# The low half of each weight tile by a negated copy and an accumulating DMA, in a one-core decoder layer

## The chip, the core and the metric

One core of one Trainium2 chip runs the program. The metric is the device time of one execution in microseconds (us). Before the change three runs took 771.84, 771.36 and 771.56 us; the median is 771.56 us.

## What is computed

One layer of a decoder, 512 tokens wide 1024, all in float32:

```
u = rms_norm(h, norm_mix_pre);  proj = u @ w_in          # 1024 -> 10*256 + 4*1024
y_a, y_b, y_c, y_d = four token mixers on slices of proj # 512 x 256 each
merged = sum_k sigmoid(gate_k) * (y_k @ w_branch[k])      # 512 x 1024
h = h + rms_norm(merged @ w_out, norm_mix_post)
u = rms_norm(h, norm_mlp_pre)
hid = square(relu(u @ w_up))                              # 512 x 4096
h = h + rms_norm(hid @ w_down, norm_mlp_post)
```

## The kernel before, in words

**Products in three parts.** Each float32 operand is split into a high half, rounded to the type that TensorE reads (float32r), and a low half, the rest. `mm3` (lines 180 to 183) makes a product of two operands from three matmuls: high by high (L181), then the two mixed ones (L182, L183). So every weight tile is needed twice, as `whi` and as `wlo`, each [128, 1024].

**Units.** The weights lie in DRAM as 132 units of [128, 1024] (512 KB) in the order of use. A unit goes through three steps. `load` (L129) sends its DMA from SyncE's queue into one of 3 `raw` buffers. `prep` (L143) takes one of 6 `whi` and one of 6 `wlo` buffers and calls `split` (L139): ScalarE copies `raw` to `whi` (L140), then VectorE writes `wlo = raw - whi` (L141). Then TensorE uses the pair, 24 matmuls of 512 columns for a unit. `unit()` (L172) prepares 4 units ahead of the one that it hands out. Units 66 and 67 go to a spare pair of buffers of another pool.

**Stages.** Ten slots of the input projection (20 units), then four gates (40 units, 8 of them of `w_branch`), with the mixers' own steps written between them; then `w_out` (8 units); then the MLP in 8 groups of 512 hidden columns. A group is `up_group`, which uses four units one after the other, and `down_group` of the group before, which holds four units together: each of its 8 output pieces takes 3 matmuls from each of the four (12 matmuls), and VectorE adds the piece to `macc` (L918). In `up_out` ScalarE applies relu (L850), VectorE squares (L851), and `split` makes the halves of `hid`.

**The end.** The last `down_group` also forms row sums (ScalarE L738, VectorE L749), the norm, the gain (GpSimd L926) and the residual, and sends the output.

**Order.** A scheduler orders each engine's instructions when the program is built, and each engine runs its own queue in order. So ScalarE's copy for a unit stands at a fixed place among its other work, and what stands behind it waits with it. GpSimd has little to do before the last group: memsets, and one cast (L250).

Of the kernel before, what the change touches and what calls it, by code (L numbers as in the profile page):

```python
# [12 lines left out]
AF = mybir.ActivationFunctionType  # L13
ALU = mybir.AluOpType
# [35 lines left out]
def tile_hybrid_trunk(ctx: ExitStack, tc: tile.TileContext, xT, xn, wts, par, bd, cst, msk, gains, out):  # L50
    nc = tc.nc
    act, dve, pool, pe = nc.scalar, nc.vector, nc.gpsimd, nc.tensor
# [15 lines left out]
    def nm(s):  # L68
        cnt[0] += 1
        return f"{s}_{cnt[0]}"  # L70
# [19 lines left out]
    def y_pair():  # L90
        r = []
        for s in ("hi", "lo"):
            r.append(yp.tile([P, 2 * T], F32R, tag="y", name=nm("y" + s)))
        return r
# [23 lines left out]

    NU = wts.shape[0]
    SPARE = (66, 67)  # L120
    spare = []
    LOADCUT = {0: ((0, 256), (256, 512), (512, D))}
    xfirst = [0, 1, 2]

    def xload(k):
        nc.sync.dma_start(xt[k // 2][:, k % 2], xT[k])

    def load(n):
        while Wt.n_load < min(n, NU):  # L129
            i = Wt.n_load  # L130
            r = rp.tile([P, D], F32, tag="raw", name=nm("raw"))
            for o, e in LOADCUT.get(i, ((0, D),)):
                if i == 0 and xfirst:
                    xload(xfirst.pop(0))
                nc.sync.dma_start(r[:, o:e], wts[i, :, o:e])
            Wt.raw[i] = r
            Wt.n_load += 1

    def split(hi, lo, src):  # L139
        act.activation(hi, src, AF.Copy)  # L140
        dve.tensor_tensor(lo, src, hi.bitcast(F32), ALU.subtract)  # L141

    def prep(n):  # L143
        while Wt.n_prep < min(n, NU):
            i = Wt.n_prep
            load(i + 1)
            r = Wt.raw.pop(i)
            if i in SPARE:
                if not spare:
                    spare.extend(up.tile([P, 2, D], F32R, tag="u", name=nm("sp")) for _ in range(2))  # L150
                hi, lo = (x_[:, i - SPARE[0]] for x_ in spare)
            else:
                hi = wp.tile([P, D], F32R, tag="whi", name=nm("whi"))
                lo = wp.tile([P, D], F32R, tag="wlo", name=nm("wlo"))
            for o, e in LOADCUT.get(i, ((0, D),)):
                if i == 0 and xorder[0] == 0:
                    xorder.pop(0)
                    xsplit(0, lambda: split(hi[:, o:e], lo[:, o:e], r[:, o:e]))
                    continue
                split(hi[:, o:e], lo[:, o:e], r[:, o:e])  # L160
                if i == 0:
                    xsplit(xorder.pop(0))
            Wt.hl[i] = (hi, lo)
            Wt.n_prep += 1
            load(i + 3)
# [6 lines left out]
    def unit():  # L172
        i = use[0]
        use[0] += 1
        prep(i + ahead[0])
        if extra:
            extra.pop(0)()
        return Wt.hl.pop(i)
# [27 lines left out]
    def xsplit(k, between=None):  # L206
        src = xt[k // 2][:, k % 2]
        g = prm("gmix", k)
        if k == 0:
            dve.tensor_scalar(U(uh, k), src, g, None, ALU.mult)  # L210
        else:
            act.activation(U(uh, k), src, AF.Copy, scale=g)  # L212
        if between:
            between()
        dve.scalar_tensor_tensor(U(ul, k), src, g, U(uh, k).bitcast(F32), ALU.mult, ALU.subtract)  # L215
# [11 lines left out]
    for k in range(4, NK):  # L227
        xload(k)
    load(3)
    prep(1)  # L230
    xsplit(3)
    prep(2)
    for k in range(4, NK):
        xsplit(k)
# [135 lines left out]
    hi, lo = y_pair()  # L370
# [688 lines left out]
```

## Time and profile before

| | |
|---|---|
| three runs, us | 771.84, 771.36, 771.56 |
| span of the profiled execution, us | 769.9 |
| TensorE (PE) busy | 756.5 us, 98% |
| VectorE (DVE) busy | 450.2 us, 58% |
| ScalarE (ACT) busy | 264.5 us, 34% |
| GpSimd (POOL) busy | 18.8 us, 2% |
| mean granted TensorE clock | 0.996 |
| DMA | 80.40 MB, mean 104 GB/s |

The profile gives the profiled execution as its span, from the first to the last instruction; the page lists no other time for it. The chain that ended last consists of PE for 95% of the span. A busy PE is one with a matmul in flight, since matmuls overlap.

### The profile page before, as it was taken

What the parts mean: (1) busy time and instruction counts of PE and PEld (TensorE: products, weight loads), DVE (VectorE), ACT (ScalarE), POOL (GpSimd) and SP (SyncE); (2) the same over time, 40 slices, a digit from 0 to 9 for tenths busy, and PEclk for the clock granted to TensorE, in tenths of its full rate; (3) what the DMA queues carried; (4) which work ended last, traced back from release to release, by engine and by line L of the source; (5) the groups of instructions that cost most, each with busy time, mean ns of one, the idle gap of its engine ahead of it and who ended that gap; (6) DMA issues with size and microseconds to landing.
All of it is one profiled execution on the core that took longest, in us unless ns stands there. A gap on an engine that the chain in (4) does not pass through costs nothing.

```text
span 769.9 us, 9006 instructions
## 1 busy us (share of the span) xinstructions
PE 756.5 (98%) x3592; PEld 636.0 (83%) x3592; DVE 450.2 (58%) x699; ACT 264.5 (34%) x375; POOL 18.8 (2%) x21
## 2 busy tenths in 40 slices
PE   8999999999999999999999999999999999999994
PEld 7888988888888888888889988888888888888883
DVE  5798246559988476465476742435354453435357
ACT  6524122337223223234242743413142231414123
POOL 1100000000000000000000000000000000000014
PEclk9999999999999999999999999999999999999998
DMA  8732223132222263233321331405142331405002
GB/s 338 247 116 98 98 94 110 56 109 83 83 82 68 97 219 110 82 102 118 109 82 56 117 104 53 139 28 163 55 140 79 109 111 34 157 28 163 28 1 109
DMA packets 23945, 80.40 MB, mean 104 GB/s; under 512 B 2784, under 2 KB 3552, under 8 KB 23904
## 3 DMA queue, kind: packets, MB, share of 16 engines
q1 hardware_dynamic: 23616, 79.67, 30.9%
q8 instruction: 28, 0.46, 0.3%
q10 hardware_dynamic: 288, 0.17, 0.1%
q14 instruction: 13, 0.11, 0.0%
HBM read 77.73 MB, written 2.10 MB: 104 GB/s over the span
## 4 chain that ended last, share of the span: by engine, by line
PE 95%; DVE 3%; DMA 1%; ACT 0%; issue 0%; DVEq 0%; ACTq 0%
PE mm L182 22%; PE mm L183 22%; PE mm L181 22%; PE sm L181 9%; PE sm L183 8%; PE sm L182 8%; PE sm L512 2%; DMA raw<-in_wts_dram 1%; DVE stat L749 1%; DVE macc L918 0%; DVE t L896 0%; PE sm L621 0%; DMA par_s<-in_par_dram 0%; PE sm L807 0%; DVE nt L762 0%
## 5 line engine op out<-in xcount | busy, mean ns | idle before, releaser
L140 ACT ACTIVATE whi<-raw 128x1024 fp32r<-128x1024 f32 (+1 forms) x132 | 136.8, 1046 | 334.0 <-PE mm L182 138.6
L141 DVE TENSOR_TENSOR wlo<-raw,whi 128x1024 fp32r<-128x1024 f32 (+1 forms) x132 | 158.7, 1207 | 135.2 <-ACT whi L140 134.8
L182 PE MATMUL mm<-ul,whi 128*128 128x512 f32 x384 | 149.3, 390 | 0.6 <-DVE ul L215 0.6
L181 PE MATMUL mm<-uh,whi 128*128 128x512 f32 x384 | 148.7, 392 | 0.9 <-ACT uh L212 0.9
L183 PE MATMUL mm<-uh,wlo 128*128 128x512 f32 x384 | 149.1, 390 | 0.0
L182 PE MATMUL mm<-u2l,whi 128*128 128x512 f32 (+1 forms) x288 | 105.2, 366 | 0.0
L183 PE MATMUL mm<-u2h,wlo 128*128 128x512 f32 (+1 forms) x288 | 105.0, 365 | 0.0
L181 PE MATMUL mm<-u2h,whi 128*128 128x512 f32 (+1 forms) x288 | 104.4, 365 | 0.0
L182 PE MATMUL sm<-wlo,hid 128*128 128x512 f32 (+1 forms) x260 | 100.3, 386 | 0.0
L183 PE MATMUL sm<-whi,hid 128*128 128x512 f32 (+1 forms) x260 | 100.3, 386 | 0.0
L181 PE MATMUL sm<-whi,hid 128*128 128x512 f32 (+1 forms) x260 | 100.0, 386 | 0.0
L182 PEld LDWEIGHTS mm<-ul,whi 128*128 128x128 f32 x384 | 72.3, 188 | 16.0 <-DVE ul L215 1.2
L181 PEld LDWEIGHTS mm<-uh,whi 128*128 128x128 f32 x384 | 72.2, 188 | 16.0 <-ACT uh L212 1.3
L183 PEld LDWEIGHTS mm<-uh,wlo 128*128 128x128 f32 x384 | 72.1, 188 | 15.0
L918 DVE TENSOR_TENSOR macc<-macc,sm 128x512 f32<-128x512 f32 (+1 forms) x57 | 38.3, 676 | 71.3 <-PE sm L183 71.3
L183 PEld LDWEIGHTS mm<-u2h,wlo 128*128 128x128 f32 x288 | 54.3, 189 | 8.8
L182 PEld LDWEIGHTS mm<-u2l,whi 128*128 128x128 f32 x288 | 54.3, 189 | 8.7
L181 PEld LDWEIGHTS mm<-u2h,whi 128*128 128x128 f32 x288 | 54.0, 189 | 8.8
L183 PEld LDWEIGHTS sm<-whi,hid 128*128 128x128 f32 x260 | 48.8, 188 | 9.9
L181 PEld LDWEIGHTS sm<-whi,hid 128*128 128x128 f32 x260 | 48.8, 188 | 9.8
L182 PEld LDWEIGHTS sm<-wlo,hid 128*128 128x128 f32 x260 | 48.8, 188 | 9.8
L851 DVE TENSOR_TENSOR s<-s 128x512 f32<-128x512 f32 x32 | 22.0, 688 | 37.8 <-ACT s L850 37.8
(242 smaller groups left out, 788.1 us busy)
## 6 DMA issues: line engine op xcount, KB each, us to landing
raw<-in_wts_dram SPq DMA_DIRECT2D x131, 512.0 KB, 3.3
t<-in_xn_dram SPq DMA_DIRECT2D x8, 512.0 KB, 8.1
xt<-in_xt_dram SPq DMA_DIRECT2D x8, 256.0 KB, 5.4
out_dram<-t SPq DMA_DIRECT2D x7, 256.0 KB, 2.0
t<-in_gains_dram SPq DMA_DIRECT2D x3, 512.0 KB, 5.9
t<-in_bd_dram SPq DMA_DIRECT2D x1, 384.0 KB, 5.4
raw<-in_wts_dram SPq DMA_DIRECT2D x2, 128.0 KB, 3.4
raw<-in_wts_dram SPq DMA_DIRECT2D x1, 256.0 KB, 4.2
```

The costliest lines, as they stand in the source:

```text
L140: act.activation(hi, src, AF.Copy)
L141: dve.tensor_tensor(lo, src, hi.bitcast(F32), ALU.subtract)
L181: pe.matmul(ps, lh, rh, start=first, stop=False)
L182: pe.matmul(ps, lh, rl, start=False, stop=False)
L183: pe.matmul(ps, ll, rh, start=False, stop=last)
L512: pe.matmul(bk[ct][:, cs].rearrange("s (h n b) -> s h n b", h=2, b=B), kk_[:, ct, cs], qo, start=True, stop=True)
L749: dve.scalar_tensor_tensor(v, stat[:, t, j : j + 1], 1.0 / D, prev, ALU.mult, ALU.add)
L851: dve.tensor_tensor(rl, rl, rl, ALU.mult)
L918: dve.tensor_tensor(m, m, ps, ALU.add)
```

## The change

From unit 6 on, 126 of the 132 units, the low half is no longer made by VectorE. ScalarE writes `whi` as before (L157 of the changed kernel). It then writes the negated copy into `wlo` (L158), rounded as `whi` is, so that `wlo` holds `-whi`. GpSimd then starts a DMA (L159) that reads the unit from DRAM a second time and adds it to `wlo`, which leaves `raw - whi` as before. The `raw` buffer is free once ScalarE has read it twice. Lines of the changed kernel behind this place are 9 higher than before (L850 is L859, L181 to L183 are L190 to L192).

```diff
@@ tile_hybrid_trunk
     SPARE = (66, 67)
+    VIA = 6
     spare = []
@@ prep
                 lo = wp.tile([P, D], F32R, tag="wlo", name=nm("wlo"))
+            if i >= VIA:
+                act.activation(hi, r, AF.Copy)
+                act.activation(lo, r, AF.Copy, scale=-1.0)
+                pool.dma_start(lo, wts[i], accum_op=ALU.add)
+                Wt.hl[i] = (hi, lo)
+                Wt.n_prep += 1
+                load(i + 3)
+                continue
             for o, e in LOADCUT.get(i, ((0, D),)):
```

The scheduler orders the changed program anew. Three places show what moved.

GpSimd's queue at the start of the program, changed kernel (`msk_s` is a mask of the token mixers, `sT` a score buffer; each `wlo` row is the accumulating DMA of one unit, unit 6 first):

```order
L259 CAST msk_s<-s_352 128x320
L159 DMA wlo_274<-in_wts_dram 128x1024
L159 DMA wlo_342<-in_wts_dram 128x1024
L159 DMA wlo_381<-in_wts_dram 128x1024
L159 DMA wlo_443<-in_wts_dram 128x1024
L159 DMA wlo_474<-in_wts_dram 128x1024
```

Before, the cast was followed by the two memsets of `sT`; these now stand behind the tenth of the DMAs.

ScalarE's queue in the last MLP group but one step before its `down_group`, kernel before: the copies of the third and fourth unit of `up_group` (5064, 5188), of the four units of the `down_group` (5218, 5260, 5290, 5330), and the relus between them (L850):

```order
L140 ACTIVATE whi_5064<-raw_5056 128x1024
L140 ACTIVATE whi_5188<-raw_5062 128x1024
L140 ACTIVATE whi_5218<-raw_5068 128x1024
L140 ACTIVATE whi_5260<-raw_5192 128x1024
L140 ACTIVATE whi_5290<-raw_5222 128x1024
L850 ACTIVATE s_5248<-mm_5186 128x512
L140 ACTIVATE whi_5330<-raw_5264 128x1024
L850 ACTIVATE s_5253<-mm_5187 128x512
```

The same place of the changed kernel, from the fourth unit of `up_group` (5305, 5306) on:

```order
L158 ACTIVATE wlo_5306<-raw_5178 128x1024
L157 ACTIVATE whi_5305<-raw_5178 128x1024
L158 ACTIVATE wlo_5337<-raw_5185 128x1024
L157 ACTIVATE whi_5336<-raw_5185 128x1024
L157 ACTIVATE whi_5379<-raw_5310 128x1024
L158 ACTIVATE wlo_5380<-raw_5310 128x1024
L157 ACTIVATE whi_5410<-raw_5341 128x1024
L158 ACTIVATE wlo_5411<-raw_5341 128x1024
L859 ACTIVATE s_5367<-mm_5303 128x512
L157 ACTIVATE whi_5451<-raw_5384 128x1024
L859 ACTIVATE s_5372<-mm_5304 128x512
L158 ACTIVATE wlo_5452<-raw_5384 128x1024
```

Each copy has its negated copy beside it, in three cases ahead of it, and the last one stands behind the second relu. Before these rows stands the same pair for the third unit of `up_group`, negated copy first.

TensorE in the last `down_group`, kernel before, where the first three output pieces (5468, 5487, 5517) wait for its fourth unit (5464, 5465):

```order
L182 MATMUL sm_5468<-wlo_5465,hid_5183 128x512
L183 MATMUL sm_5468<-whi_5464,hid_5185 128x512
L182 MATMUL sm_5487<-wlo_5465,hid_5183 128x512
L183 MATMUL sm_5487<-whi_5464,hid_5185 128x512
L181 MATMUL sm_5517<-whi_5464,hid_5183 128x512
L182 MATMUL sm_5517<-wlo_5465,hid_5183 128x512
L183 MATMUL sm_5517<-whi_5464,hid_5185 128x512
```

And in the changed kernel (fourth unit 5589, 5590):

```order
L191 MATMUL sm_5594<-wlo_5590,hid_5300 128x512
L192 MATMUL sm_5594<-whi_5589,hid_5302 128x512
L191 MATMUL sm_5613<-wlo_5590,hid_5300 128x512
L192 MATMUL sm_5613<-whi_5589,hid_5302 128x512
L191 MATMUL sm_5643<-wlo_5590,hid_5300 128x512
L192 MATMUL sm_5643<-whi_5589,hid_5302 128x512
L192 MATMUL sm_5662<-whi_5472,hid_5302 128x512
L190 MATMUL sm_5662<-whi_5589,hid_5300 128x512
L191 MATMUL sm_5662<-wlo_5590,hid_5300 128x512
L192 MATMUL sm_5662<-whi_5589,hid_5302 128x512
```

Four pieces wait for the fourth unit instead of three, and the first of them ends 10 matmuls later in TensorE's queue. In the other MLP groups TensorE's order is the same in both kernels.

## Rows read from the trace of the kernel before

**Rows 1.** The page, sections 1 and 2: busy time, granted clock and DMA by slice.
```profile
PE 756.5 (98%) x3592; PEld 636.0 (83%) x3592; DVE 450.2 (58%) x699; ACT 264.5 (34%) x375; POOL 18.8 (2%) x21
...
PEclk9999999999999999999999999999999999999998
DMA  8732223132222263233321331405142331405002
```
**Rows 2.** The page, section 5: the two halves of the weights' split.
```profile
L140 ACT ACTIVATE whi<-raw 128x1024 fp32r<-128x1024 f32 (+1 forms) x132 | 136.8, 1046 | 334.0 <-PE mm L182 138.6
L141 DVE TENSOR_TENSOR wlo<-raw,whi 128x1024 fp32r<-128x1024 f32 (+1 forms) x132 | 158.7, 1207 | 135.2 <-ACT whi L140 134.8
```
**Rows 3.** One MLP group: stretch; busy PE, PEld, DVE, ACT, POOL; clock; DMA share; GB/s.
```profile
604.50:648.00 43.50, 43.50 (x194) 36.02 (x193) 20.00 (x25) 12.54 (x16) 0.00 (x0) 1.00 0.29 97
```
**Rows 4.** Timeline of ACT in that group: start, duration, what, idle before.
```profile
604.54 2.96 ACT L140 ACTIVATE whi<-raw 128x1024 fp32r<-128x1024 f32 x3 [16.31 <-PE sm L183]
610.29 1.06 ACT L140 ACTIVATE whi<-raw 128x1024 fp32r<-128x1024 f32 x1 [2.79 <-DMA raw<-in_wts_dram]
613.44 1.06 ACT L140 ACTIVATE whi<-raw 128x1024 fp32r<-128x1024 f32 x1 [2.08 <-DMA raw<-in_wts_dram]
616.78 0.60 ACT L850 ACTIVATE s<-mm 128x512 f32<-128x512 f32 x1 [2.29 <-PE mm L183]
617.29 1.06 ACT L140 ACTIVATE whi<-raw 128x1024 fp32r<-128x1024 f32 x1
618.25 0.58 ACT L850 ACTIVATE s<-mm 128x512 f32<-128x512 f32 x1
```
**Rows 5.** Timeline of PE: the first and tenth matmul behind the group's `up_group`.
```profile
628.14 0.39 PE L181 MATMUL sm<-whi,hid 128*128 128x512 f32 x1
...
630.41 0.39 PE L182 MATMUL sm<-wlo,hid 128*128 128x512 f32 x1
```
**Rows 6.** DMA: the queue of the loads; their issues, with us to landing.
```profile
q1 hardware_dynamic: 23616, 79.67, 30.9%
...
raw<-in_wts_dram SPq DMA_DIRECT2D x131, 512.0 KB, 3.3
```
**Rows 7.** Busy time by stretch: the fullest microsecond of DMA; its last two numbers.
```profile
12.00:13.00 1.00, 0.59 (x2) 0.16 (x2) 1.00 (x2) 1.00 (x3) 0.00 (x0) 1.00 1.05 430
```
**Rows 8.** What the queue of the loads waits for, longest first.
```profile
SPq L135 <- DVE wlo L141: 574.2, 117, 19.5
```
**Rows 9.** Timeline of POOL at the start.
```profile
21.06 0.45 POOL L250 CAST msk_s<-s 128x320 uint8<-128x320 f32 x1 [18.27 <-DMA s<-in_msk_dram]
21.45 1.85 POOL L422 MEMSET sT<- 128x1024 f32 x2
```
**Rows 10.** Timeline of ACT: the copy of unit 6.
```profile
24.87 1.07 ACT L140 ACTIVATE whi<-raw 128x1024 fp32r<-128x1024 f32 x1 [0.25 <-DMA raw<-in_wts_dram]
```
**Rows 11.** Matmuls of L183 from 30 to 60 us: duration ns, first and last start.
```profile
L183 PE MATMUL mm<-uh,wlo x28: 389/389/389, 41.1 to 59.4; 128*128 128x512 f32 x28
```
**Rows 12.** The tail, timeline of DVE at 744 and 760 us.
```profile
744.17 1.88 DVE L918 TENSOR_TENSOR macc<-macc,sm 128x512 f32<-128x512 f32 x3 [5.02 <-PE sm L183]
...
760.26 0.42 DVE L918 TENSOR_TENSOR macc<-macc,sm 128x256 f32<-128x256 f32 x1
```
**Rows 13.** Busy time by stretch: PE's end, and its granted clock behind that.
```profile
758.00:760.00 2.00, 1.02 (x9) 0.81 (x7) 1.97 (x5) 0.93 (x3) 1.25 (x2) 1.00 0.00 0
...
762.00:764.00 2.00, 0.00 (x0) 0.00 (x0) 1.92 (x2) 0.57 (x4) 1.90 (x2) 0.93 0.32 122
764.00:766.00 2.00, 0.00 (x0) 0.00 (x0) 1.68 (x7) 0.71 (x2) 0.31 (x1) 0.50 0.38 140
```

## The prediction

> **What bounds the kernel now.** I read the page first. TensorE is busy for 98% of the span, at the full granted clock from the first slice to the last but one, while DVE has 58% and ACT 34% [rows 1]. Then I read the busy time by stretch. A whole MLP group, 43.5 us long, has PE busy for 43.50 us, with DVE at 20.00 and ACT at 12.54 [rows 3]. Nothing that VectorE does there holds TensorE up. The two views together say that a gain on DVE is worth nothing between the first matmuls and PE's end at about 759.3 us [rows 13], and that the only question is whether the new way of making `wlo` keeps every tile ahead of TensorE.
>
> The timeline of ACT shows how far ahead the tiles are now. When a `down_group` lets go of its four units, ACT copies three at once at 604.54, the next at 610.29 and 613.44 when their loads land, and the sixth at 617.29 behind the first relu [rows 4]. These are the third and fourth unit of `up_group`, then the four of the next `down_group`. TensorE starts on those four at 628.14 and reads the low half of the fourth at 630.41, ten matmuls later [rows 5]. VectorE's 1.2 us for a low half fits in easily.
>
> **What the change takes away and adds.** A measurement of this kernel tells about 0.2% (1.5 us) from no change. The sum is made against the span of 769.9 us; the runs' median of 771.56 us is 1.7 us above it, and I carry that over.
>
> - *VectorE*: 126 subtractions at 1.207 us go [rows 2], 152 of its 450 us. They stood beside TensorE, so the gain is 0.
> - *ScalarE*: 126 negated copies, each like the copy to `whi`, at 1.046 us [rows 2]: 132 us more than 264.5 [rows 1], 396 us or 51%. ACT sat idle 334 us ahead of its copies [rows 2], which covers this. In the MLP group 8.4 us join 12.54 in 43.5 us [rows 3]. Cost 0. Behind a late copy stand the relus (L859) that empty TensorE's `mm` banks; there are two pairs of banks, so a relu may come a slot (10.9 us) late.
> - *SyncE's loads*: the next load waited for VectorE's subtraction 117 times [rows 8]; it will wait for the negated copy. For the first of the three tiles at 604.54 that is 0.3 us sooner, for the third about 1 us later. The tile loaded then is wanted at 617.29 [rows 4], so 0.
> - *GpSimd*: 126 DMA issues in a queue that was empty. The first stands behind the cast that ends at 21.51 [rows 9]; unit 6 is copied at 24.87 [rows 10], negated by about 27, and first read by a matmul of L183 at 41.1 [rows 11]. 14 us of cover; cost 0.
> - *The tail*: DVE's last stretch starts at 744.17 with three pieces [rows 12]. In the new order the first piece of that batch ends 10 matmuls later, at 0.227 us each (630.41 − 628.14 over ten, [rows 5]), 2.3 us. PE still ends at the same place, and DVE's queue, at 760.26 just behind PE's end [rows 12, 13], has gaps that take some of it back. Bounds 0 and 2.3; I take +1.
> - *The accumulating DMA*: the one term that decides. No row of before shows one.
>
> **The price X of an accumulating DMA.** X is the time that one takes of the 16 DMA engines. The load queue used 30.9% of 769.9 us for 79.67 MB [rows 6], so 1.57 us for a 512 KB load; at the fullest, 430 GB/s [rows 7], it would be 1.22 us. The least for X is one such pass. An add needs the old `wlo` too, so two passes, 2.44 to 3.13, are the nearest price. If each pass had to land before the next began, it would be twice the 3.3 us from issue to landing [rows 6], 6.6 us. I take 2.8, the middle of two passes, because one load of this size is the nearest row and the operation reads two tiles.
>
> Now the group, in the new order of ACT. With 0.95 us a copy from 604.54, `wlo` stands negated at about 605.6, 607.5 and 609.4, then at 612.3 and 615 (loads landing as in [rows 4]), and the last at 619.8, behind both relus. So six accumulations are issued from 605.6, and all must have landed by 630.4. From issue to landing a load takes 3.3 us, 1.7 of it beyond its transfer [rows 6], so the engines have 605.6 to 628.7, 23.1 us. In that time they also carry three loads that the group needs (4.7 us) and up to three more for the next (9.4 in all). The group stalls for 6X plus these, less 23.1:
>
> - X = 2.44: 14.6 + 4.7 to 9.4, a stall of 0 to 0.9 us;
> - X = 2.8: 16.8 + 4.7 to 9.4, 0 to 3.1 us;
> - X = 3.13: 18.8 + 4.7 to 9.4, 0.4 to 5.1 us.
>
> I take 2 us, since both queues will be served in turn for most of the time, and there are 7 such groups: 14 us. With the tail, 771.6 + 15 = **787 us**. This case's own range is 772 to 808 (7 × 5.1 + 1).
>
> The Trainium skill, "DMA: Bandwidth & Descriptors", section "Issuing engines are not separate DMA queues", says that transfers started by SyncE and GpSimd run on the same 16 engines and interleave. If the queues had engines of their own, the sum would be 16.8 us against 23.1 and the kernel would stand at 772.6; no run here shows two large queues at once yet.
>
> In the projection and gate stages a unit is used every 5.44 us (24 × 0.227), and X + 1.57 is 4.4 us, 80% of that. I put no stall there.
>
> **Rivals.**
>
> *Hidden after all.* If X is below 2.28 (or 3.07 when the extra loads give way), no group stalls, and only the tail is left: 771.6 + 1 = 772.6 us, between 770.5 and 774. For it speaks that even two passes at 430 GB/s, 2.44, stall by 0.9 us at most; against it, that 430 GB/s stands in one microsecond of the start only [rows 7], and that the loads average 1.57 us [rows 6]. The Trainium skill, "Collectives: The Full Stack", section "The bandwidth ceiling: the fold count and why AG ≠ RS ≠ AR", states that a reducing transfer reads two sources through the same ring and so gets half of about 31 GB/s for each engine. By that page X is an estimate of 2.1 us and the sum 12.7 + 9.4, under 23.1, so the time would be 772.6 us. No row of before tests it.
>
> *Queue-bound.* If X is above 5.44 − 1.57 = 3.9 us, the accumulations can't keep up even in the projection stages. At the upper end, 6.6 us, about 58 units there (6 to 63) lose 1.16 us each, 67 us, and 7 groups lose 6 × 6.6 − 23.1 = 16.5 each, 115 us: 771.6 + 182 + 1 = 955 us. At X = 4.2 it would be about 7 × 11.5 + 58 × 0.3 = 98, so 870. Nothing in the trace speaks against it but that loads move fast; the adding itself and GpSimd's own issuing have no row. Long stalls would cost more than their length: once PE was done the granted clock fell from 1.00 to 0.93 and then 0.50, the lower level of 1.2 GHz [rows 13].
>
> *Faster.* DVE's freedom could shorten the tail only. Its queue ends a piece less than 1 us behind PE [rows 12, 13], so the gain stays under 1 us; 770.8 at best, which counts as no change unless the new order does better than I see.
>
> **How the numbers follow.** Stalled groups (787) 0.38; hidden (772.6) 0.32; queue-bound (870 to 955) 0.26; faster 0.04. Most of the hidden case lies within 0.2% of 771.56, 0.28 of its 0.32, the rest above. So faster 0.04, same 0.28, slower 0.38 + 0.26 + 0.04 = 0.68. The range starts at 770.5, where the hidden case starts, and reaches to 900: it leaves out the faster end and somewhat over half of the queue-bound case, together about 0.18.
>
> **What would show it.** Right: PE waits in the MLP groups only, on L191 (`wlo`), released by the accumulating DMA, 7 times and 1 to 5 us each, at the start of a `down_group`; a second DMA queue with 66 MB and 35 to 50% of the engines; DVE near 298 us, ACT near 396. Wrong: PE busy throughout, or the queue's share under 30% (hidden); PE waits at every unit, or accumulations that lie behind one another without a gap (queue-bound); waits of PE on `mm` banks or on ACT, which would say that the negated copies are in the way.

## The result and the profile after

The changed kernel takes **790.62 us** (median of 4 runs, 789.37 to 791.93) against 771.58 us for the kernel before (771.36 to 771.84): ratio 1.0247, 95% interval [1.0233, 1.0261]. The forecast was 787.0, and the mechanism forecast is the one that the trace shows. The profiled execution took 791.93 us, with a span of 790.2, which is 20.3 us more than the span of before.

The page of the changed kernel, sections 1 to 3, 5 and 6:

```profile
PE 762.1 (96%) x3592; PEld 637.8 (81%) x3592; DVE 305.1 (39%) x573; ACT 380.5 (48%) x501; POOL 128.2 (16%) x147
...
DMA  9898798788686798898943957839395693939622
...
q0 software_dynamic: 18144, 66.07, 44.9%
q1 hardware_dynamic: 23616, 79.67, 29.9%
...
L159 POOL DMA_DIRECT2D wlo<-in_wts_dram x124 | 107.2, 864 | 606.2 <-ACT wlo L158 580.0
...
raw<-in_wts_dram SPq DMA_DIRECT2D x131, 512.0 KB, 7.8
wlo<-in_wts_dram POOLq DMA_DIRECT2D x124, 512.0 KB, 8.4
```

Beside [rows 1], DVE lost 145 us of work and ACT gained 116, and neither shows in the time. The DMA row is where to look: of the 23 slices that stood at 2 or 3, 16 now stand at 7 to 9. The new queue q0 moves 66 MB and takes 44.9% of the engines, so one accumulating DMA takes 0.449 × 790.2 / 126 = **2.82 us** of all 16. The loads' queue q1 takes what it took before, 0.299 × 790.2 × 0.524 / 79.67 = 1.55 us a load, but a load now lands 7.8 us behind its issue instead of 3.3 [rows 6].

What TensorE waits for in the changed kernel (waiting engine and line, releaser: us in total, times, longest):

```profile
PE sm L191 <- DMA wlo<-in_wts_dram: 12.5, 6, 3.0
PE sm L190 <- ACT whi L157: 1.5, 1, 1.5
```

The first row is what was forecast: matmuls of a low half in `down_group`, released by the accumulating DMA. The stalls end at 504.68 (2.43 us), 551.65 (1.54), 598.03 (2.55), 644.52 (1.36), 691.38 (3.02) and 736.82 (1.61). They are long and short in turn, as the sixth accumulation of a group goes out 18.9, 17.9, 19.1, 17.8, 20.7 and 17.8 us behind the first; why these alternate stays open. There are six and not seven: the first `down_group`, at 456, waits for nothing. The first of its six accumulations go out at 428.5, 432.1 and 434.5, where every later group starts three within 4 us, and its last goes out at 449.5, 9 us ahead of the matmul that reads it (4.2 to 7.1 us in the groups that stall). That this is why it does not stall is read from the trace and was not tested. The second row is one wait at the start of `w_out`, at 364.27, which the forecast had not.

How a stall comes about is read from the group that ends in this one:

```profile
598.03 0.80 PE L191 MATMUL sm<-wlo,hid 128*128 128x512 f32 x1 [2.55 <-DMA wlo<-in_wts_dram]
```

First ACT's timeline of the changed kernel (start, duration, what, idle before): three copies wait for a load.

```profile
573.98 1.04 ACT L157 ACTIVATE whi<-raw 128x1024 fp32r<-128x1024 f32 x1
577.75 1.06 ACT L157 ACTIVATE whi<-raw 128x1024 fp32r<-128x1024 f32 x1 [2.72 <-DMA raw<-in_wts_dram]
...
583.46 1.06 ACT L157 ACTIVATE whi<-raw 128x1024 fp32r<-128x1024 f32 x1 [3.70 <-DMA raw<-in_wts_dram]
...
586.87 1.06 ACT L157 ACTIVATE whi<-raw 128x1024 fp32r<-128x1024 f32 x1 [0.92 <-DMA raw<-in_wts_dram]
```

POOL's timeline of the same group, the first and the last of six accumulations:

```profile
570.58 0.86 POOL L159 DMA_DIRECT2D wlo<-in_wts_dram  x1 [19.24 <-ACT wlo L158]
...
589.66 0.86 POOL L159 DMA_DIRECT2D wlo<-in_wts_dram  x1 [3.03 <-ACT wlo L158]
```

The DMA view of 569 to 598 us, queue by queue (packets, MB, share of the 16 engines):

```profile
q0 software_dynamic: 909, 3.33, 61.1%
q1 hardware_dynamic: 981, 3.61, 32.3%
```

Six accumulations go out from 570.58 to 589.66, and the stall ends at 598.03, 8.4 us behind the last issue. In these 29 us the new queue takes 17.7 us of the engines (0.611 × 29; the 3.33 MB are the six units and a third of a seventh) and the loads 9.4 (0.323 × 29), and by the view's 40 slices the engines do not rest from 573 on. The forecast had 6 × 2.8 = 16.8 and 4.7 to 9.4. What it did not say is the loop in between: the loads share the engines with the accumulations, so ACT waits for `raw` (2.72, 3.70 and 0.92 us), and so the next accumulations go out late. The sixth leaves 20.4 us behind the group's first copy (569.23), where the forecast had it 15.3 us behind (604.54 to 619.8).

### The profile page after: what moved, and what is told of

Same layout as the page of the kernel before. It is cut to its first block, busy times and chain, and to the rows that moved or that the text cites. A ratio compares the mean times of both kernels' runs of the same rounds, so it can differ in the third digit from the quotient of the medians.

```text
span 790.2 us, 9239 instructions
## 1 busy us (share of the span) xinstructions
PE 762.1 (96%) x3592; PEld 637.8 (81%) x3592; DVE 305.1 (39%) x573; ACT 380.5 (48%) x501; POOL 128.2 (16%) x147
## 3 DMA queue, kind: packets, MB, share of 16 engines
q0 software_dynamic: 18144, 66.07, 44.9%
q1 hardware_dynamic: 23616, 79.67, 29.9%
HBM read 143.79 MB, written 2.10 MB: 185 GB/s over the span
## 4 chain that ended last, share of the span: by engine, by line
PE 74%; issue 15%; DMA 5%; POOL 2%; DVE 2%; ACT 1%; SPq 0%; DVEq 0%; POOLq 0%; ACTq 0%
PE mm L191 18%; PE mm L192 18%; PE mm L190 18%; PE sm L191 5%; PE sm L190 5%; PE sm L192 5%; DMA wlo<-in_wts_dram 3%; POOL wlo L159 2%; DMA raw<-in_wts_dram 2%; PE sm L521 2%; DVE t L905 1%; DVE stat L758 1%; PE sm L630 0%; DVE nt L771 0%; PE sm L816 0%
## 5 line engine op out<-in xcount | busy, mean ns | idle before, releaser
L157 ACT ACTIVATE whi<-raw 128x1024 fp32r<-128x1024 f32 x124 | 130.9, 1056 | 182.3 <-issue 88.2
L159 POOL DMA_DIRECT2D wlo<-in_wts_dram x124 | 107.2, 864 | 606.2 <-ACT wlo L158 580.0
L158 ACT ACTIVATE wlo<-raw 128x1024 fp32r<-128x1024 f32 x124 | 129.7, 1046 | 123.9 <-PE sm L191 111.5
L190 PE MATMUL mm<-uh,whi 128*128 128x512 f32 x384 | 149.2, 392 | 0.8 <-ACT uh L221 0.8
L192 PE MATMUL mm<-uh,wlo 128*128 128x512 f32 x384 | 148.3, 390 | 0.0
L191 PE MATMUL sm<-wlo,hid 128*128 128x512 f32 (+1 forms) x260 | 102.2, 394 | 12.5 <-DMA wlo<-in_wts_dram 12.5
L192 PE MATMUL mm<-u2h,wlo 128*128 128x512 f32 (+1 forms) x288 | 105.1, 366 | 0.0
L190 PE MATMUL mm<-u2h,whi 128*128 128x512 f32 (+1 forms) x288 | 104.5, 366 | 0.0
L192 PE MATMUL sm<-whi,hid 128*128 128x512 f32 (+1 forms) x260 | 101.2, 390 | 0.0
L190 PE MATMUL sm<-whi,hid 128*128 128x512 f32 (+1 forms) x260 | 101.0, 390 | 0.0
L190 PEld LDWEIGHTS mm<-uh,whi 128*128 128x128 f32 x384 | 72.1, 188 | 16.1 <-ACT uh L221 1.2
L192 PEld LDWEIGHTS mm<-uh,wlo 128*128 128x128 f32 x384 | 72.4, 188 | 15.2
L192 PEld LDWEIGHTS mm<-u2h,wlo 128*128 128x128 f32 x288 | 54.3, 189 | 8.6
L190 PEld LDWEIGHTS mm<-u2h,whi 128*128 128x128 f32 x288 | 54.0, 189 | 8.7
L190 PEld LDWEIGHTS sm<-whi,hid 128*128 128x128 f32 x260 | 49.5, 190 | 10.3
```

The lines of the kernel that those rows point to most:

```text
L157: act.activation(hi, r, AF.Copy)
L158: act.activation(lo, r, AF.Copy, scale=-1.0)
L159: pool.dma_start(lo, wts[i], accum_op=ALU.add)
L190: pe.matmul(ps, lh, rh, start=first, stop=False)
L191: pe.matmul(ps, lh, rl, start=False, stop=False)
L192: pe.matmul(ps, ll, rh, start=False, stop=last)
```

## The experiments

The question was whether the time goes into the engines' time of the add (theory 1), into the way through GpSimd's queue (theory 2), or into ScalarE's extra copies (theory 3), and whether the traffic alone or the waiting for it stalls TensorE. All times are medians against runs of the kernel before on the same chip (771.3 to 771.4 us).

**1. The DMA without the add.**

```diff
-                pool.dma_start(lo, wts[i], accum_op=ALU.add)
+                pool.dma_start(lo, wts[i])
```

> GpSimd's DMA writes the unit over wlo instead of adding it to the negated half, so the low halves are not low halves: that part of the computation is left out. Queues, issues, copies, waits and bytes stay those of the change; only the add goes. Theory 1 (the engines' time of the add): the second queue falls from 44.9% to some 20 to 26% of the engines, 1.2 to 1.6 us a unit instead of 2.82; a group then wants 6 x 1.57 + 9.4 = 18.8 us of the 23.1 us window, no PE wait on L191 above 0.3 us is left, and the time is 771.5 to 774 us. Theory 2 (the way through GpSimd's queue is long in itself: issue, landing, one more link in the chain from raw to wlo): the waits stay at 1 us or more in most groups, 780 to 790 us. Theory 3 (ScalarE's two copies and its order are in the way): about 790 us, as the change.

Measured: 772.29 us, ratio 1.0012 [1.0002, 1.0021]. No PE wait in the MLP. Its page, sections 3, 5 and 6:

```profile
q0 software_dynamic: 18144, 66.07, 24.7%
...
L159 POOL DMA_DIRECT2D wlo<-in_wts_dram x124 | 65.6, 529 | 633.4 <-ACT wlo L158 612.9
...
raw<-in_wts_dram SPq DMA_DIRECT2D x131, 512.0 KB, 4.0
wlo<-in_wts_dram POOLq DMA_DIRECT2D x124, 512.0 KB, 4.7
```

The same bytes in the same packets through the same queue take 0.247 × 770.6 / 126 = 1.51 us, against 2.82 with the add. So the add costs 1.3 us of the engines for each unit, and without it the six fit into the window. 18 of the 19 us hang on the add, and the way through GpSimd's queue, which this run keeps, is not the cause.

The run takes away one thing more. The first accumulation of a group, which starts on idle engines (a load follows 0.7 us later), lands 6.8 to 7.0 us behind its issue in the change and 3.4 to 3.7 us here (the last group aside). So an add is slow to land by itself, before any queue forms. Which of the two makes the stall can be estimated for the group above. TensorE wants the sixth accumulation 24.9 us behind the issue of the first (570.58 to 595.48). Here the sixth goes out 14.4 us behind the first (562.07 to 576.47; 14.4 to 14.9 in five of the six groups, 17.6 in one), in the change 19.1. Issued as early as here and landing in the change's 8.3 us, it would be there after 22.7 us, without a stall; issued as late as in the change and landing in 6.9 us, it would come after 26.0 us, a stall of 1.1 instead of 2.55. By this estimate the slow landing alone makes no stall: it takes the copies that the shared engines make late. That bears out theory 1.

**2. The second DMA left out.**

```diff
-                pool.dma_start(lo, wts[i], accum_op=ALU.add)
```

> The second DMA is left out, so that wlo holds only the negated high half: the adding of the unit to it is left out of the computation. ScalarE's two copies per unit and the late loads' order stay. Theories 1 and 2: no PE wait on a wlo or whi above 0.5 us in the MLP groups, raw loads land again in 3 to 4 us (7.8 in the change), 771.6 to 773 us; also the 1.5 us wait at the start of w_out goes. Theory 3 (ScalarE): 785 us or more, with PE waits on ScalarE's copies.

Measured: 772.48 us, ratio 1.0016 [1.0006, 1.0025]; raw loads land in 3.3 us again, and no wait on a weight tile is left behind the first matmuls. ScalarE's 126 extra copies (380.0 us busy) cost TensorE nothing. Theory 3 falls. Of the 1.2 us that are left, the last matmul's start has 0.3 us and the tail behind it 0.8.

**3. Every second unit.**

```diff
-            if i >= VIA:
+            if i >= VIA and i % 2 == 0:
```

> Only the even units from 6 on get their low half by the accumulating DMA, the odd ones by VectorE's subtraction. Theory 1: a group wants 3 x 2.82 + 9.4 = 17.9 us of the 23.1 us window, so no stall is left: 772 to 774 us, the second queue at some 22%. Theory 2 (each accumulation is late by its own latency, whatever the load on the engines): the groups whose last tile is an even unit still wait 1 to 3 us, 776 to 785 us. Theory 3: ScalarE has half of its added work, 778 to 784 us.

Measured: 777.49 us, ratio 1.008 [1.0064, 1.0095]: 6 us too slow for theory 1, but not where any theory put it. What TensorE waits for in this run, first row:

```profile
PE sm L521 <- DVE t L587: 4.0, 2, 3.3
```

The MLP groups have no stall at all. This does not speak against theory 2 as it is put here (each accumulation late by its own latency): the fourth unit of every `down_group` has an odd number (79, 87, up to 131), so no group's last tile is an accumulated one, neither here nor in run 4. What speaks against it is the estimate at run 1. The time goes in a mixer, at 203 and 212 us: the 800th matmul starts at 172.44 (173.21 in the kernel before), the 1200th at 257.44 (251.28), and the last 6.0 us late. The wait is of another kind (a score's matmul behind VectorE's piece `t`). In this build PE's 16 score matmuls at 203 stand behind 4 matmuls of `yhi`, where the kernel before has 12 (and the change none, but there VectorE has no subtraction in the way). That VectorE's remaining subtractions and the altered order together make this wait is read from the trace and was not tested by itself; run 4 tests only where it comes from.

**4. Every second unit in the MLP only.**

```diff
-            if i >= VIA:
+            if i >= VIA and (i < 68 or i % 2 == 0):
```

> As the change up to unit 67, then the accumulating DMA for the even units only: three of the six of a group. The sum: 3 x 2.82 + 9.4 = 17.9 of 23.1, no stall in the MLP; with the first 68 units as in the change and not alternating, the PE waits of 4 us on VectorE's piece of the mixer that the run with all even units had should be gone too: 772 to 774.5 us. If those waits come back, they are not of the alternation in the mixers.

Measured: 774.47 us, ratio 1.0041 [1.0026, 1.0055]. Neither the mixer's waits nor any in the MLP; the last matmul starts at 758.81, against 758.74 in the kernel before. So three accumulations of six leave no stall, and the waits of run 3 belong to the alternation in the mixers. Most of the 3 us left lie behind the last store's issue, where SyncE waits for TensorE's sequencer at the program's end (SyncE's queue's waits, this run):

```profile
SPq L1064 <- PEq L1064: 3.5, 2, 3.0
```

In every other run this row has 0.6 to 1.1 us. It has no part in the mechanism; why it is long here stays open.

**5. Five of six.**

```diff
-            if i >= VIA:
+            if i >= VIA and (i < 68 or i % 8 != 3):
```

> As the change, but the last of the eight units of an MLP group gets its low half from VectorE: five accumulations fall into the 23.1 us before a down group instead of six. The forecast's sum: 5 x 2.82 + 4.7 to 9.4 = 18.8 to 23.5, so 0 to 0.4 us of stall a group, 772.3 to 776 us. If it is not this sum that decides but the raw loads that land late behind the accumulations, the last unit's copy waits as before and the PE waits move to VectorE's or ScalarE's half of it: 782 us or more.

Measured: 773.97 us (773.78 to 777.03), ratio 1.0045 [1.0028, 1.0062]. What TensorE waits for:

```profile
PE sm L190 <- ACT whi L157: 1.7, 1, 1.7
PE sm L233 <- DVE spt L476: 1.1, 1, 1.1
PE sm L191 <- DMA wlo<-in_wts_dram: 1.0, 2, 0.8
```

The unit that VectorE makes here (`i % 8 == 3`) is the fourth of an `up_group`, the second of the group's six copies. It is not the unit that the stalled matmuls waited for: that one, the fourth of the `down_group`, is still an accumulated one, except in the last group. One accumulation less in a group takes the stalls from 12.5 us to 1.0. The sum of the forecast gives 0 to 0.4 a group for this case; two groups stall for 0.75 and 0.26, the others not. The window is the right place to count, and it is nearly full at five. (The profile is of the execution of 775.89 us, one of the two longer ones of five; its 1.7 us at `w_out` have nothing to do with the window.)

**6. The traffic without the waiting.** The kernel before, with the accumulations added from unit 72 on into buffers that nothing reads:

```diff
+            if i >= 72:
+                for o in range(0, D, T):
+                    sc = dead[dn[0] % 4]()
+                    dn[0] += 1
+                    pool.tensor_copy(sc[:, :1], lo[:, o : o + 1].bitcast(F32))
+                    pool.dma_start(sc, wts[i, :, o : o + T], accum_op=ALU.add)
```

> The kernel before, every low half by VectorE; from unit 72 on GpSimd also starts two accumulating DMAs of 512 columns for each unit, into buffers that nothing reads, each behind a one-column copy of that unit's low half, so that they come when the change's come. The MLP has the change's traffic, and no matmul waits for it. Theory A (the matmuls stall because they wait for the accumulation itself): 771.3 to 773 us, raw loads land in 6 us or more in the groups, but VectorE's way has the slack for it. Theory B (the traffic alone is enough, since the raw loads behind it land late): 780 us or more, PE waits on VectorE's or ScalarE's copies at the down groups. The second queue should take about 2.8 us of the engines for each unit of 512 KB in either.

Measured: 771.36 us, ratio 1.0000 [0.999, 1.0009]. No PE wait in the MLP. Its page, section 3, first:

```profile
q0 software_dynamic: 17280, 31.46, 23.7%
```

The queue takes 0.237 × 769.6 / 60 = 3.04 us a unit, no less than in the change, and TensorE does not notice. How near the traffic comes to the change's is seen in the MLP alone, 460 to 760 us, beside run 9, which has the change's accumulations in the MLP only. The DMA view of this run:

```profile
q0 software_dynamic: 14671, 26.71, 51.5%
q1 hardware_dynamic: 7355, 25.72, 24.0%
...
raw<-in_wts_dram SPq DMA_DIRECT2D x47, 512.0 KB, 6.6
```

And of run 9:

```profile
q0 software_dynamic: 7329, 26.71, 46.3%
q1 hardware_dynamic: 6775, 24.67, 21.8%
...
raw<-in_wts_dram SPq DMA_DIRECT2D x47, 512.0 KB, 9.1
```

The engines are fuller than in run 9, 75.5% against 68.1%. The loads land later than in the kernel before (3.3 us) but sooner than in run 9. Each accumulation here first waits until one of its four buffers is free, so that at most two units' worth are under way at once, which may be why. So full engines alone do not stall this kernel: what stalls it is that a matmul waits for the accumulation itself. Theory A holds, for loads that land in 6.6 us; loads of 9.1 us without the wait were not tried.

**7. The addend from SBUF.**

```diff
-                pool.dma_start(lo, wts[i], accum_op=ALU.add)
+                pool.dma_start(lo, r, accum_op=ALU.add)
```

> The accumulating DMA reads the unit from its raw buffer in SBUF instead of from DRAM; the sum stays. Theory A (an accumulation costs two passes of the engines, one to read the old tile and one to write the new, wherever the other operand lies): the second queue takes 2.4 to 3.2 us a unit as in the change (2.82), stalls and 785 to 800 us; the raw buffer is held until it lands, which may add late loads. Theory B (the price is two streams out of DRAM side by side with the loads): 1.2 to 1.8 us a unit, and 771.5 to 776 us.

Measured: 807.23 us (801.86 to 808.29), ratio 1.0451 [1.0415, 1.0487]. The profile is of the execution of 801.86 us. Its page, section 3:

```profile
q0 software_dynamic: 18144, 66.07, 45.6%
```

What TensorE waits for in it, first row:

```profile
PE sm L191 <- DMA wlo<-raw: 18.0, 6, 4.1
```

What the loads' queue waits for in it, first row:

```profile
SPq L136 <- DMA wlo<-raw: 658.9, 121, 18.9
```

With half of the HBM reads gone (77.73 MB instead of 143.79), an accumulation still takes 0.456 × 800.1 / 126 = 2.90 us. The price is that of the add on the engines and not of the second stream out of DRAM. From issue to landing the place does matter: the first accumulation of a group lands in 4.5 to 4.8 us here, against 6.8 to 7.0 in the change. The stalls are longer all the same, 18.0 us. `raw` is now held until the DMA has read it, and the loads wait for that 121 times, where in the change they waited for ScalarE's copies; that this makes the stalls longer is read from the trace and was not tested by itself.

**8. The stages ahead of the MLP alone, twice.**

```diff
-            if i >= VIA:
+            if VIA <= i < 68:
```

> The accumulating DMA is used for units 6 to 67 only (the mixer and gate stages); the MLP's 64 units are split by VectorE as before the change. All theories that put the cost in the MLP groups: 790.6 - 12.5 of stalls - 5 of low clock and order = 773 us (772 to 774.5), with the 1.5 us wait at the start of w_out and the 0.3 to 0.5 us of the mixers kept. If the stages ahead of the MLP carry a cost that the PE rows hide: 778 us or more.

> The kernel of the run with units 6 to 67 only, once more, for its profile: its times lay in two heaps, 771.4 to 771.6 and 773.1 to 774.2, and the profile that was taken is of the lower one, without a wait at the start of w_out. If that wait (1.54 us in the change) is what separates the heaps, a profile of the upper heap shows it, 1 to 2 us on L190 behind the copy to whi; if not, the upper heap's extra time is elsewhere. Theory: upper heap, 773 us, with the wait.

Measured: 773.36 us (7 runs, 771.43 to 774.19), ratio 1.0023 [1.0011, 1.0035], and 772.59 in the single run of the repeat. No PE wait in the MLP in either. The profile of the execution that took 771.64 us has no wait at `w_out`, the one of 772.59 has 0.63 us there (its timeline of PE):

```profile
362.53 0.96 PE L190 MATMUL sm<-whi,yhi 128*128 128x512 f32 x3 [0.63 <-ACT whi L157]
```

The change has 1.54 us at this place, run 5 had 1.66. So the stages before the MLP cost 0.1 to 2.9 us from run to run, 2.1 by the median. The two profiles' spans differ by 1.0 us (770.8 and 769.8), and 0.8 of it lies at `w_out`: the matmul there starts 1.01 us behind the one before it, where 0.23 is the usual step. How long it waits goes by how late one load lands: ACT stands at the copy to `sp` until `raw` has landed (6.63 us in the repeat, 5.34 in the first, 7.54 in the change), and the copy to `whi` that `w_out` needs is queued behind it. The times lie in two heaps, two at 771.4 to 771.6 us and five at 773.1 to 774.2, and the repeat's lies between them, so that this wait explains all of the upper one is likely and not shown.

**9. The MLP alone.**

```diff
-    VIA = 6
+    VIA = 68
```

> The accumulating DMA for units 68 to 131 only; everything ahead of the MLP as before the change. If the MLP groups carry all but the wait at the start of w_out: the six waits on L191 come back, 12 to 13 us in total and two falls of the clock, PE starts the MLP within 0.5 us of the kernel before (2.2 us later in the change), and the time is 790.6 - 2 = 788.5 us (787.5 to 790). If the load of the earlier stages had helped to make the MLP late: 785 us or less.

Measured: 788.96 us, ratio 1.0224 [1.0207, 1.0241]. What TensorE waits for, first row:

```profile
PE sm L191 <- DMA wlo<-in_wts_dram: 11.6, 6, 2.7
```

Six stalls again, of 2.70, 1.46, 2.20, 1.42, 2.40 and 1.44 us, in the same alternation of long and short as in the change. The two parts of the change add up: 17.6 us for the MLP (788.96 − 771.34) and 2.1 for the rest (773.36 − 771.3) make 19.7, where the whole measured 19.0.

No version here beats the kernel before, in which TensorE is busy for 98% of the span.

## Why the prediction was right, step by step

The likeliest case, *stalled groups*, is what happened; 790.62 lies 3.6 us above its 787.0 and well inside its own range.

- **The price X.** Forecast 2.8 us, as the middle of two passes; measured 2.82, and 2.76 to 3.04 in the other runs with an add (runs 3 to 9, worked out as above). The packets' times of the two queues overlap a little (their share comes to 1.01 to 1.10 in the full stretches shown at the end), so these figures are a few per cent too high. Run 1 measured the one pass, 1.51. The argument "an add needs the old `wlo` too" was right by its number; that the engines read the old tile is not seen in any row. Run 7 shows that the price does not depend on where the other operand lies.
- **The hidden rival** fell by this price. It needed X below 2.28. By the Trainium skill, "Collectives: The Full Stack", section "The bandwidth ceiling: the fold count and why AG ≠ RS ≠ AR", X was estimated at 2.1 us. The halving that the page states for a reducing transfer of a collective is borne out in kind here (2.82 / 1.51 = 1.87). The rate of 31 GB/s for each engine is not reached even by the plain DMA of run 1 (512 KB over 16 engines in 1.51 us is 21.7 GB/s for each), and by that the estimate came out too low.
- **One set of engines for both queues.** The loads' landing rose from 3.3 to 7.8 us and q1's own share of the engines stayed, so the two queues do hinder each other. That is what the Trainium skill, "DMA: Bandwidth & Descriptors", section "Issuing engines are not separate DMA queues", says, and the trace agrees.
- **The window.** 6X + 4.7 to 9.4 against 23.1: the group above used 17.7 + 9.4, the forecast's upper end, and the stalls came out at 1.36 to 3.02 us, with 12.5 / 6 = 2.1 as their mean against the forecast 2. Runs 4 and 5 move the number of accumulations in the window, and the stalls follow: six 12.5 us, five 1.0, three none (with three, the last unit is VectorE's too). That the mean came so near is in part luck: 2 was picked out of 0 to 3.1. And the window's end was set by a load's 1.7 us from transfer to landing, where the first accumulation of a group shows 4.1 (6.9 less 2.8).
- **The number of groups.** The term that was off: "there are 7 such groups". Six stalled, 12.5 us instead of 14.
- **What was left out of the sum.** Three terms of the profiled span's +20.3 us have no place in the forecast: TensorE at a lower granted clock behind two of the stalls, 3 us (below); the wait at `w_out`, 1.5; and what a wait costs beyond its own length, 2. The last is read from the starts of the matmuls:

```profile
549.71 0.39 PE L190 MATMUL sm<-whi,hid 128*128 128x512 f32 x1
551.65 0.50 PE L191 MATMUL sm<-wlo,hid 128*128 128x512 f32 x1 [1.54 <-DMA wlo<-in_wts_dram]
551.98 0.40 PE L192 MATMUL sm<-whi,hid 128*128 128x512 f32 x1
```

A wait is counted from the end of the matmul before it, 0.39 us behind its start, but the next one would have started after 0.23; and behind the wait the first step is 0.33 instead of 0.23. That makes 0.3 us for each of the seven waits. With the stalls, 12.5, a start that is 0.5 us later, and the tail, 0.8, the sum is 20.3. So the forecast's 15 us came near the measured 19 because the stalls were sized about right; terms that it had at nothing make up the rest. It named the clock as a price of long stalls, and gave it no term in this case.

- **The covers.** DVE 305 us against 298 forecast, ACT 380 against 396, both with room; run 2, at 1.2 us above the kernel before, shows that ScalarE's part costs next to nothing. The load at the start of `w_out` is where one cover was too thin: "I put no stall there" holds for the projections and gates, but ACT's in-order queue carried a late load into a copy that was wanted at once.
- **The tail.** Forecast +1, bounds 0 and 2.3. The span runs 11.9 us beyond the start of the last matmul instead of 11.2 (790.2 − 778.25, 769.9 − 758.74). In runs 1 and 2, which have no stall, the same stretch is 11.9 and 12.0 us, and they stand 1.0 and 1.2 us above the kernel before.
- **Queue-bound** fell with X below 3.9. Its upper end was summed too low: at X = 6.6 the loads' 1.57 us were left out, which the sum for 4.2 has. With them the 58 units lose 2.7 us each and the groups up to 25.9, and the time would be some 1,110 us and not 955. Nothing else hangs on it.
- **Faster** had nothing to win, as [rows 1] said: TensorE was busy for 98% of the span.

## What to carry to other kernels

In these runs a 512 KB DMA that adds costs the transfer engines nearly twice the time of one that copies (2.82 against 1.51 us), whether the addend comes from DRAM or from SBUF, and while it runs the loads land later (7.8 us instead of 3.3). Count it as engine time in the narrowest stretch between the release of buffers and their next use, not over the whole span: here 75% of the engines on average (44.9 + 29.9) was too much because six of them fell into 23 us, and a matmul waited for the last. And work taken off an engine that nobody waits for is worth nothing, as the 145 us less of VectorE show, while the wait that replaces it may stand on the path.

## What the runs showed of the hardware

- GpSimd is busy for 864 ns with the issue of one accumulating DMA and for 529 ns with that of a plain one of the same shape (run 1).
- An accumulating DMA of 512 KB from DRAM that starts on idle engines lands 6.8 to 7.0 us behind its issue, from SBUF 4.5 to 4.8 us (run 7), and a plain one from DRAM 3.4 to 3.7 us (run 1).
- The granted clock behind a stall did not go by the stall's length. In the changed kernel it fell after the stalls of 2.43 and 2.55 us, and stayed at 1.00 after the longest, 3.02; each time TensorE had been busy for 43.8 us or more before. Busy time by stretch behind the stalls at 504.68 and at 691.38 (stretch, busy PE, clock, DMA share, GB/s):

```profile
504.00:506.00 2.00, 1.32 (x4) 0.82 1.10 254
506.00:508.00 2.00, 2.00 (x6) 0.50 1.01 313
508.00:510.00 2.00, 2.00 (x8) 0.82 1.10 238
510.00:512.00 2.00, 2.00 (x10) 1.00 0.20 41
...
690.00:692.00 2.00, 0.62 (x3) 1.00 1.01 219
692.00:694.00 2.00, 2.00 (x10) 1.00 1.04 258
```

0.50 is the lower of the two levels, 1.2 GHz. By the clock, the fall cost 0.36 + 1.00 + 0.36 = 1.7 us behind the stall at 504.68, and 1.4 behind the one at 598.03 (0.50 for 2 us, 0.78 for 2 us); by the starts of the matmuls it is 1.6 and 1.3. In run 7 it came behind five of the six stalls, of 2.16 to 4.09 us, and not behind the one of 3.31. What decides it stays open.
